# A two-layer hybrid decoder trunk: the mixers' table of chunks, side jobs and counts is replaced by another

## The chip, the core and the metric

The kernel runs on one core of a Trainium2 chip. The core has a matrix engine (TensorE: PE in the profile, PEld for its weight loads), a vector engine (VectorE, DVE), a scalar engine (ScalarE, ACT), a general engine (GpSimd, POOL) and a queue that issues DMA transfers (SyncE, SP). Each takes its own instructions in order and waits for the others by semaphores. The metric is the device time of one execution in microseconds. TensorE writes into PSUM, from which the other engines read; a PSUM buffer can be written again only when its readers are done.

## The reference

Two layers, each of three sub-layers on x (256 tokens by 1024): a gated feed-forward network (hidden width 2816) at half weight, a mixer, and a second feed-forward network at half weight. Each is wrapped in two RMS norms, x + r * post(f(pre(x))). The mixer adds two branches, each behind a sigmoid gate, and sends the sum through one output product:

```
# gated DeltaNet branch, 8 heads of 128, chunks of 64 tokens
qkv = silu(conv4(qkv));  q, k = l2norm(q), l2norm(k)
beta = sigmoid(b);  g = -exp(a_log) * softplus(a + dt_bias);  G = cumsum(g)
a_mat = strictly lower part of (k k^T * exp(G_i - G_j) * beta)
u, w  = (I + a_mat)^-1 [v * beta, k * beta * exp(G)]
per chunk: v_new = u - w state;  o = q exp(G) state + (q k^T * decay) v_new
           state = state * exp(G_last) + (k exp(G_last - G))^T v_new
o = rmsnorm(o) * silu(z)
# Conformer branch: h = a * sigmoid(gate); h = silu(layernorm(conv31(h) + dw_b))
```

All of it is float32.

## The kernel before, in words

**Weights.** Each weight matrix comes in pieces of 128 rows by 1024 columns, loaded by SP (`raw`, four buffers, line 272). ScalarE rounds a piece to `whi` (line 276) and VectorE or GpSimd makes the rest, `wlo = raw - whi` (line 280); rings of 8 hold both. A product is three matmuls, high by high, high by low, low by high. The class `Stream` decides when each step is issued; the set `POOL` says by piece number whose `wlo` GpSimd makes (53 of a mixer's pieces).

**Order of the work.** The program is straight-line. While the main line writes matmuls, a counter (`Lanes.tick`, line 212) goes up, one tick per few matmuls: in an FFN's output product, three. Side jobs (`step` of a generator up to its next `yield`) are issued when the counter has reached their due time. `DELAY` gives for each job the ticks before its first step and between the following ones, `AFTER` and `LATE` after which other jobs, and how many ticks later, it may start. `PLAN` lists the 17 column chunks in which a mixer's input product is done (g: the Conformer's gate pairs, k, q, v, z: those of DeltaNet, a and b: the branch gates, ka and kb: k with the small decay columns) and the jobs that are added when a chunk is done. `CFG` holds priorities and lags. The fillers (the taps of the long convolution on VectorE, the steps of the inverse on GpSimd) have no counts: they are issued while an engine's modelled clock is less than a set time ahead of TensorE's modelled one. `vector_us` and `pool_us` (lines 85 to 95) give these clocks their durations. What each engine does in which order is thus fixed when the program is built.

**The jobs that matter below.**
- `pre0` (lines 449 to 484): at the end of a sub-layer's output product, when the first 128 tokens are through their post norm, x times the norm weight goes into `xw`, and TensorE transposes it in two groups of four, `tr<-cst,xw`. It runs at five boundaries: FFN to mixer twice (there xw waits for the norm factor `rstd`), and mixer to FFN and FFN to FFN, three in all.
- `inv` (lines 995 to 1022): the triangular blocks are inverted on GpSimd in 31 pairs of steps on `iu`, behind `xin`, the decays and `dt`; two DMAs write the result to a buffer `dU`, eight bring it back as `u`.
- `merge` (lines 1023 to 1071): TensorE transposes u (`gd<-cst,u`) and puts the blocks together; the scans `s0`, `s1` need it.
- `cn` (lines 1268 to 1292): the layer norm behind the long convolution. Four transposes of h (`hT`) go into one PSUM buffer `tr`; VectorE takes the statistics (`bns`, `mv`), GpSimd the power -0.5 (`lnr`), VectorE writes `xhat` out of PSUM, and TensorE transposes `xhat` back; ScalarE makes `cf` of that. `tr` and the merge's `gd` have three PSUM buffers between them, the products' `mm` four.

In the profile one line, L124, stands for all VectorE and GpSimd operations, L171 for ScalarE's, L144 for matmuls and L150 for transposes; all lie 12 higher in the changed kernel.

Of the kernel before, what the change touches and what calls it, by code (L numbers as in the profile page):

```python
# [35 lines left out]


PLAN = [
# [4 lines left out]
]  # L43

DELAY = {
# [12 lines left out]
}  # L58

AFTER = {  # L60
# [9 lines left out]

FILL = (("c3", "c2", "c1", "c0"), ("inv",))

LATE = {"inv": 20, "cn": 12, "sim0": 5, "sim1": 6, "merge": 7, "dts": 14}

POOL = {*range(7, 10), *range(11, 14), 16, *range(18, 21), 22, 23, 25, *range(29, 33), 35, 36, 38, 39, *range(41, 45), *range(47, 50), 51, 53, 55, 58, 60, 61, 63, *range(65, 69), *range(70, 73), 77, 78, 85}

CFG = dict(stat=1000, conv=50, ev=300, tok=4, st=4, post=-800, pre=1000, fin=None, turn=100, tokens=-100, glu=100, dec=200, dts=500, kt=300, vt=0, qt=50, inv=1000, sim=100, merge=-400, scan=50, norm=-800, onorm=-100, yt=-400, w=50, tails=4, ahead=1.5, lag=6, free=3, aheadp=3, lag2=3, bias=2, held=1)

KIND = {"f_g0": "glu", "f_g1": "glu", "f_g2": "glu", "f_g3": "glu", "decays": "dec", "dts": "dts", "kt0": "kt", "kt1": "kt",
        "vt0": "vt", "vt1": "vt", "qt0": "qt", "qt1": "qt", "qs": "qt", "inv": "inv", "sim0": "sim", "sim1": "sim",  # L80
# [2 lines left out]


def vector_us(name, size, k):
    return 0.1 + size / 960.0


def pool_us(name, size, k):
# [88 lines left out]
class Lanes:  # L178
# [24 lines left out]
    def ready(self, job):  # L203
        late = LATE.get(job[1], 0)
        return job[2] or all(self.done.get(name, self.now) + late <= self.now and name in self.done for name in AFTER.get(job[1], ()))
# [6 lines left out]
    def tick(self):  # L212
# [5 lines left out]
        for job in list(self.jobs):  # L218
            if job in self.jobs and not any(job[1] in f for f in FILL) and job[0] <= self.now and self.ready(job):
                self.step(job)  # L220
        for eng, names, ahead in zip(self.engines, FILL, (CFG["ahead"], CFG["aheadp"])):
            while eng.at < self.pe.at + ahead:
# [109 lines left out]
def trunk(ctx: ExitStack, tc: tile.TileContext, x_in, wfirst, consts, feat, pch, tokp,  # L332
# [70 lines left out]
    for l in range(depth):  # L403
        side += [False] * 66 + [i in POOL for i in range(90)] + [False] * 66
        pieces += [w1i[l, i] for i in range(44)] + [w1o[l, i] for i in range(22)]
# [1101 lines left out]
```

## Time and profile before

| | |
|---|---|
| median of three runs | 1353.26 us (1352.9 to 1353.55) |
| profiled execution | span 1349.7 us; the page gives no other time of it, and the timed median lies 3.6 us over the span |
| TensorE busy | 1327.1 us in 7259 matmuls and transposes |
| VectorE, ScalarE, GpSimd busy | 933.8, 732.3 and 445.5 us |
| mixer 1 and mixer 2 | about 184 to 488 us and 853 to 1156 us |

A line of the page gives the code's line, the engine, the operation and its tiles (out<-in), the shapes and the count. A bracket at the end of a row of a timeline is the time for which the engine sat idle before it, and what ended that. SPq is the queue that issues DMAs.

### The profile page before, as it was taken

How to read it: one execution, taken by the hardware profiler on the slowest of the kernel's cores; microseconds unless marked ns; L12 is line 12 of the kernel's file. 1: busy time of each engine (PE TensorE's matmuls, PEld its weight loads, DVE VectorE, ACT ScalarE, POOL GpSimd, SP SyncE). 2: the span in 40 equal slices, each digit the busy share in tenths (PEclk: the TensorE clock that was granted, in tenths of full speed). 3: DMA queues.
4: the chain of work that ended last, by engine and by line, in shares of the span. 5: the costliest groups of instructions: out<-in, count | busy, mean ns of one | idle time of the engine just before them, and what ended most of it. 6: DMA issues, size and time to landing. Idle time of an engine off the chain costs nothing.

```text
span 1349.7 us, 20220 instructions
## 1 busy us (share of the span) xinstructions
PE 1327.1 (98%) x7259; PEld 1128.0 (84%) x7259; DVE 933.8 (69%) x1594; ACT 732.3 (54%) x1175; POOL 445.5 (33%) x374
## 2 busy tenths in 40 slices
PE   9999999999999999999999999999999999999998
PEld 7888889997787888888888888899977878888886
DVE  6676455999966776665576654579999666766553
ACT  7545447675555545544455543577656564555541
POOL 0111017798744201111011120277986431011110
PEclk9999999999999999999999999999999999999999
DMA  8878746562634666776468775465545446477861
GB/s 274 287 239 260 249 156 210 166 211 96 206 110 153 225 218 222 276 249 221 155 219 280 265 235 186 146 231 172 173 138 183 143 139 234 154 261 247 273 212 39
DMA packets 115652, 273.76 MB, mean 203 GB/s; under 512 B 24768, under 2 KB 48352, under 8 KB 115552
## 3 DMA queue, kind: packets, MB, share of 16 engines
q1 hardware_dynamic: 115264, 272.40, 61.5%
q8 instruction: 57, 0.93, 0.3%
q14 instruction: 43, 0.35, 0.1%
q10 hardware_dynamic: 288, 0.07, 0.0%
HBM read 256.68 MB, written 15.75 MB: 202 GB/s over the span
## 4 chain that ended last, share of the span: by engine, by line
PE 81%; DVE 11%; ACT 3%; DMA 2%; issue 1%; POOL 1%; DVEq 0%; POOLq 0%; SPq 0%; ACTq 0%
PE mm L144 75%; DVE cacc L124 4%; PE gd L144 3%; DVE c L124 3%; DVE wlo L124 2%; PE tr L150 2%; DMA raw<-mw 2%; ACT whi L171 1%; DVE at L124 1%; ACT dt L171 1%; ACT sg L171 0%; DMA raw<-w2i 0%; DVE ssk L124 0%; DVE qk L124 0%; POOL rk L124 0%
## 5 line engine op out<-in xcount | busy, mean ns | idle before, releaser
L144 PE MATMUL mm<-whi,xt 128*128 128x512 f32 (+1 forms) x2048 | 647.6, 391 | 3.0 <-ACT qT L171 2.2
L171 ACT CAST whi<-raw 128x1024 fp32r<-128x1024 f32 (+2 forms) x448 | 458.8, 1035 | 316.8 <-PE mm L144 173.8
L124 DVE TENSOR_TENSOR wlo<-raw,whi 128x1024 fp32r<-128x1024 f32 (+2 forms) x342 | 427.2, 1264 | 190.0 <-ACT whi L171 183.5
L144 PEld LDWEIGHTS mm<-whi,xt 128*128 128x128 f32 x2048 | 382.3, 188 | 82.3 <-ACT qT L171 3.0
L144 PE MATMUL mm<-wlo,xt 128*128 128x512 f32 (+1 forms) x1024 | 396.4, 387 | 0.1
L124 POOL TENSOR_TENSOR wlo<-raw,whi 128x1024 fp32r<-128x1024 f32 (+1 forms) x106 | 250.5, 2379 | 142.5 <-ACT whi L171 140.0
L144 PEld LDWEIGHTS mm<-wlo,xt 128*128 128x128 f32 x1024 | 192.6, 188 | 37.6 <-DVE wlo L124 1.3
L144 PE MATMUL mm<-whi,act 128*128 128x512 f32 x704 | 218.3, 390 | 0.0
L124 POOL TENSOR_TENSOR act<-way,act 128x512 fp32r<-128x512 f32 x44 | 79.1, 1798 | 396.1 <-ACT act L171 385.9
L124 DVE SCALAR_TENSOR_TENSOR cacc<-hT,pc,cacc 128x254 f32<-128x254 f32 (+28 forms) x464 | 179.5, 472 | 0.2
L144 PE MATMUL mm<-xt,whi 128*128 128x256 f32 x960 | 175.5, 285 | 0.8 <-ACT qT L171 0.6
L144 PEld LDWEIGHTS mm<-whi,act 128*128 128x128 f32 x704 | 132.2, 188 | 27.4
L144 PEld LDWEIGHTS mm<-xt,whi 128*128 128x128 f32 x960 | 149.4, 192 | 1.9 <-ACT qT L171 0.9
L144 PE MATMUL mm<-wlo,act 128*128 128x512 f32 x352 | 137.0, 389 | 0.0
L144 PE MATMUL mm<-xt,wlo 128*128 128x256 f32 x480 | 135.9, 283 | 0.0
L171 ACT ACTIVATE ag<-mm,rstd 128x256 f32<-128x256 f32 x88 | 41.7, 474 | 100.0 <-PE mm L144 80.5
L144 PEld LDWEIGHTS mm<-xt,wlo 128*128 128x128 f32 x480 | 92.0, 192 | 0.0
L124 DVE SCALAR_TENSOR_TENSOR ag<-mm,rstd,ag 128x256 f32<-128x256 f32 x88 | 42.3, 481 | 58.7 <-ACT ag L171 58.4
L144 PEld LDWEIGHTS mm<-wlo,act 128*128 128x128 f32 x352 | 66.1, 188 | 13.6
L124 POOL TENSOR_TENSOR rpost<-ss,exp 128x1 f32<-128x1 f32 x12 | 6.5, 538 | 193.8 <-DVE ss L124 193.8
L171 ACT ACTIVATE jk<-mm 128x512 f32<-128x512 f32 x24 | 14.3, 598 | 60.4 <-PE mm L144 60.4
L124 DVE SCALAR_TENSOR_TENSOR c<-mm,pc,c 128x255 f32<-128x255 f32 (+2 forms) x108 | 43.7, 478 | 2.6 <-ACT c L171 2.6
(187 smaller groups left out, 1148.3 us busy)
## 6 DMA issues: line engine op xcount, KB each, us to landing
raw<-mw SPq DMA_DIRECT2D x168, 512.0 KB, 3.8
raw<-w2i SPq DMA_DIRECT2D x88, 512.0 KB, 4.8
raw<-w1i SPq DMA_DIRECT2D x84, 512.0 KB, 4.9
raw<-w1o SPq DMA_DIRECT2D x44, 512.0 KB, 4.7
raw<-w2o SPq DMA_DIRECT2D x44, 512.0 KB, 4.3
way<-way SPq DMA_DIRECT2D x176, 64.0 KB, 1.8
way<-way SPq DMA_DIRECT2D x44, 256.0 KB, 4.8
wbc<-feat SPq DMA_DIRECT2D x13, 512.0 KB, 4.9
```

The source lines that it names most:

```text
L124: r = op(out, *a, **k)
L144: r = self.eng.matmul(o, w, x, **k)
L150: r = self.eng.transpose(*a)
L171: r = op(*a, **k)
```

## The change

Only tables and two constants of a model change: the order of the chunks (q0/q1, g2/g3 and b0/b1 trade places), the chunk at which nine side jobs are added, the tick counts of nearly all jobs, which jobs wait how long behind others, the pieces whose `wlo` GpSimd makes (again 53 a mixer), `free`, which ends the fixed order of VectorE's taps one chunk sooner, and VectorE's modelled duration, 0.14 us instead of 0.1 us plus the size term for steps of more than 40 elements and 0.085 us for smaller ones. The two new keys of `CFG` are read nowhere. Every engine issues the same instructions as before, in another order.

```diff
--- before.py
+++ after.py
@@ -36,25 +36,37 @@
 
 
 PLAN = [
-    ("g0", ["f"]), ("k1", ["f", "sim1"]), ("ka", ["f", "decays", "kt1", "dts"]), ("g1", ["f", "c0"]),
-    ("kb", ["f", "sim0", "kt0", "inv", "c1"]), ("g3", ["f", "c3"]), ("g2", ["f"]), ("v1", ["f", "vt1", "c2"]),
-    ("q0", ["f", "qt0", "s1"]), ("q1", ["f", "qt1", "qs", "cn"]), ("v0", ["f", "vt0"]), ("z0", ["s0"]),
-    ("z1", ["merge"]), ("a0", ["cn1"]), ("b0", []), ("b1", ["on0"]), ("a1", ["on"]),
+    ("g0", ["f"]),
+    ("k1", ["f", "sim1"]),
+    ("ka", ["f", "decays", "kt1", "dts", "c1"]),
+    ("g1", ["f", "c0", "kt0"]),
+    ("kb", ["f", "inv"]),
+    ("g2", ["f", "sim0"]),
+    ("g3", ["f"]),
+    ("v1", ["f", "vt1", "c2", "c3", "cn", "vt0"]),
+    ("q1", ["f", "qt1", "s1", "qs"]),
+    ("q0", ["f", "qt0"]),
+    ("v0", ["f"]),
+    ("z0", ["cn1"]),
+    ("z1", ["merge"]),
+    ("a0", ["s0"]),
+    ("b1", ["on0"]),
+    ("b0", []),
+    ("a1", ["on"]),
 ]
 
 DELAY = {
-    "first": (1, 1, 2, 2, 2, 2, 2), "ffn": (3, 0, 12), "pre0": (10, 7, 8, 4, 5, 3), "pre1": (15, 16, 0, 13, 8),
-    "yt0": (10, 0, 10, 10, 26), "yt1": (10, 2, 0, 3, 3), "f_g0": (3, 0, 2, 9, 1), "f_g1": (5, 1, 1, 1),
-    "c0": (0, 16, 0), "f_k1": (0, 1, 3, 1, 1, 3), "f_ka": (3, 0, 3), "decays": (12, 4, 2, 15, 4),
-    "dts": (50, 3, 0, 0, 19, 19), "kt1": (18, 3, 4, 1, 4), "sim1": (39, 0, 1, 6, 8, 15, 14, 8), "f_kb": (0, 0, 8),
-    "kt0": (4, 1, 4, 0, 4), "sim0": (16, 3, 8, 1, 3, 2, 8, 0), "inv": (76, 4, 9, 0, 14, 16, 9, 1),
-    "f_g2": (0, 1, 0, 1), "c1": (7, 0), "f_g3": (0, 1, 3, 1, 1, 1, 1), "f_v0": (1, 0, 1, 1, 0, 0, 0),
-    "vt0": (20, 0, 0, 20, 0, 37, 6, 0), "c3": (19, 20, 24, 44), "f_v1": (0, 1, 3, 0, 1, 2),
-    "vt1": (56, 12, 18, 5, 17, 2, 3, 8), "c2": (6, 0, 0, 0), "f_q0": (0, 0, 3, 1, 1, 0),
-    "merge": (4, 3, 2, 2, 2, 3, 2, 2), "qt0": (6, 0, 4, 0, 1, 0, 30, 3), "qt1": (0, 10, 28, 21, 28, 0, 17, 14),
-    "f_q1": (1, 1, 3, 1, 0, 0, 2), "qs": (0, 31, 31, 24, 19), "s0": (15, 6, 0, 0, 17, 17, 25),
-    "s1": (11, 5, 3, 6, 1, 1), "cn": (52, 20, 4, 30, 3, 0, 41, 8), "on0": (13, 5, 5, 0),
-    "on": (1, 21, 0, 0, 5, 1, 16, 16), "cn1": (0, 0, 4, 0, 6, 3, 0, 1),
+    "first": (1, 1, 2, 2, 2, 2, 2), "ffn": (3, 0, 12), "pre0": (8, 7, 3, 30, 1, 4), "pre1": (15, 0, 12, 1, 0),
+    "yt0": (10, 1, 11, 24, 0), "yt1": (10, 11, 30, 8, 12), "f_g0": (3, 3, 0, 13, 9), "f_g1": (7, 1, 0, 12), "c0":
+    (0, 8, 8), "f_k1": (4, 0, 9, 0, 4, 3), "f_ka": (3, 1, 0), "decays": (12, 4, 2, 15, 4), "dts": (49, 2, 1, 2, 12,
+    25), "kt1": (14, 3, 4, 0, 3), "sim1": (20, 0, 5, 0, 20, 29, 18, 1), "f_kb": (4, 0, 5), "kt0": (12, 0, 8, 0, 3),
+    "sim0": (18, 6, 12, 0, 3, 4, 12, 30), "inv": (75, 3, 3, 0, 14, 6, 9, 0), "f_g2": (1, 0, 3, 6), "c1": (10, 12),
+    "f_g3": (6, 3, 3, 1, 16, 4, 0), "f_v0": (0, 0, 1, 1, 4, 4, 0), "vt0": (6, 0, 19, 34, 0, 45, 3, 0), "c3": (14,
+    23, 9, 32), "f_v1": (0, 0, 6, 0, 1, 9), "vt1": (56, 12, 12, 4, 18, 10, 7, 8), "c2": (14, 15, 2, 1), "f_q0": (0,
+    8, 3, 0, 0, 8), "merge": (4, 3, 0, 6, 1, 3, 0, 2), "qt0": (3, 0, 12, 1, 0, 1, 7, 6), "qt1": (12, 6, 25, 33, 32,
+    1, 20, 13), "f_q1": (9, 1, 0, 1, 0, 0, 0), "qs": (0, 11, 28, 10, 15), "s0": (0, 0, 0, 0, 16, 30, 29), "s1": (38,
+    5, 0, 8, 16, 10), "cn": (52, 1, 4, 30, 6, 0, 26, 8), "on0": (16, 7, 5, 3), "on": (0, 19, 0, 0, 13, 1, 2, 16),
+    "cn1": (12, 0, 0, 2, 2, 6, 1, 16),
 }
 
 AFTER = {
@@ -70,11 +82,11 @@
 
 FILL = (("c3", "c2", "c1", "c0"), ("inv",))
 
-LATE = {"inv": 20, "cn": 12, "sim0": 5, "sim1": 6, "merge": 7, "dts": 14}
-
-POOL = {*range(7, 10), *range(11, 14), 16, *range(18, 21), 22, 23, 25, *range(29, 33), 35, 36, 38, 39, *range(41, 45), *range(47, 50), 51, 53, 55, 58, 60, 61, 63, *range(65, 69), *range(70, 73), 77, 78, 85}
-
-CFG = dict(stat=1000, conv=50, ev=300, tok=4, st=4, post=-800, pre=1000, fin=None, turn=100, tokens=-100, glu=100, dec=200, dts=500, kt=300, vt=0, qt=50, inv=1000, sim=100, merge=-400, scan=50, norm=-800, onorm=-100, yt=-400, w=50, tails=4, ahead=1.5, lag=6, free=3, aheadp=3, lag2=3, bias=2, held=1)
+LATE = {"inv": 15, "cn": 10, "sim0": 3, "sim1": 6, "merge": 7, "dts": 15, "vt0": 6, "kt1": 3, "vt1": 0, "qt0": 5, "kt0": 0, "s1": 3, "s0": 0, "qt1": 0}
+
+POOL = {7, 8, 9, 10, 12, 18, 19, 20, 22, 23, 25, 27, 30, 32, 35, 36, 38, 39, 41, 42, 43, 46, 47, 49, 51, 53, 54, 55, 58, 61, 63, 65, 66, 67, 68, 70, 71, 72, 76, 83, 85}
+
+CFG = dict(stat=1000, conv=50, ev=300, tok=4, st=4, post=-800, pre=1000, fin=None, turn=100, tokens=-100, glu=100, dec=200, dts=500, kt=300, vt=0, qt=50, inv=1000, sim=100, merge=-400, scan=50, norm=-800, onorm=-100, yt=-400, w=50, tails=4, ahead=1.5, lag=6, free=4, aheadp=3, lag2=3, bias=2, held=1, dv=0.14, ds=0.085)
 
 KIND = {"f_g0": "glu", "f_g1": "glu", "f_g2": "glu", "f_g3": "glu", "decays": "dec", "dts": "dts", "kt0": "kt", "kt1": "kt",
         "vt0": "vt", "vt1": "vt", "qt0": "qt", "qt1": "qt", "qs": "qt", "inv": "inv", "sim0": "sim", "sim1": "sim",
@@ -83,7 +95,7 @@
 
 
 def vector_us(name, size, k):
-    return 0.1 + size / 960.0
+    return (0.14 if size > 40 else 0.085) + size / 960.0
 
 
 def pool_us(name, size, k):
```

On TensorE, end of the first FFN, output product (`act` is the gated hidden layer, `cst` the identity that a transpose multiplies by). Before:

```order
540 L144 MATMUL mm<-wlo,act 128x512
541 L144 MATMUL mm<-whi,act 128x512 x2
542 L144 MATMUL mm<-wlo,act 128x512
543 L144 MATMUL mm<-whi,act 128x512
544 L150 MATMUL tr<-cst,xw 128x128 x4
545 L144 MATMUL mm<-whi,act 128x512
```

and in the changed kernel:

```order
536 L156 MATMUL mm<-wlo,act 128x512
537 L156 MATMUL mm<-whi,act 128x512 x2
538 L156 MATMUL mm<-wlo,act 128x512
539 L156 MATMUL mm<-whi,act 128x512
540 L162 MATMUL tr<-cst,xw 128x128 x4
541 L156 MATMUL mm<-whi,act 128x512
```

The rows before these are the same pattern of matmuls in both; the first four transposes stand four rows, six matmuls, earlier. The same holds at the other boundaries.

On GpSimd, last third of the inverse in mixer 1 (`iu<-iu,ia` forms a product, `iu<-iu` subtracts it). Before:

```order
82 L124 TENSOR_TENSOR iu<-iu 128x10x12
83 L124 TENSOR_TENSOR iu<-iu,ia 128x121
84 L124 TENSOR_TENSOR iu<-iu 128x11x11
85 L124 TENSOR_TENSOR iu<-iu,ia 128x110
86 L124 TENSOR_TENSOR iu<-iu 128x11x10
87 L124 TENSOR_TENSOR iu<-iu,ia 128x108
88 L124 TENSOR_TENSOR iu<-iu 128x12x9
89 L124 TENSOR_TENSOR iu<-iu,ia 128x96
90 L124 TENSOR_TENSOR iu<-iu 128x12x8
91 L124 TENSOR_TENSOR iu<-iu,ia 128x91
92 L124 TENSOR_TENSOR iu<-iu 128x13x7
93 L124 TENSOR_TENSOR iu<-iu,ia 128x78
```

and in the changed kernel:

```order
85 L136 TENSOR_TENSOR iu<-iu 128x11x11
86 L136 TENSOR_TENSOR wlo<-raw,whi 128x1024
87 L136 TENSOR_TENSOR iu<-iu,ia 128x110
88 L136 TENSOR_TENSOR iu<-iu 128x11x10
89 L136 TENSOR_TENSOR iu<-iu,ia 128x108
90 L136 TENSOR_TENSOR iu<-iu 128x12x9
91 L136 TENSOR_TENSOR iu<-iu,ia 128x96
92 L136 TENSOR_TENSOR iu<-iu 128x12x8
93 L136 TENSOR_TENSOR iu<-iu,ia 128x91
94 L136 TENSOR_TENSOR iu<-iu 128x13x7
95 L136 TENSOR_TENSOR wlo<-raw,whi 128x1024
96 L136 TENSOR_TENSOR iu<-iu,ia 128x78
```

Two splits of weights now stand here; between the first and the last step on `iu` there are five, where there were two. On SP, between the two `dU` transfers and the eight `u` transfers, one weight load stands now and two stood before.

On TensorE, the norm behind the long convolution in mixer 1, before (the first eight hT transposes stand at 1410 and 1411, 15 matmuls ahead of row 1423):

```order
1417 L144 MATMUL mm<-wlo,xt 128x512
1418 L144 MATMUL mm<-whi,xt 128x512 x2
1419 L144 MATMUL mm<-wlo,xt 128x512
1420 L144 MATMUL mm<-whi,xt 128x512 x2
1421 L144 MATMUL mm<-wlo,xt 128x512
1422 L144 MATMUL mm<-whi,xt 128x512
1423 L150 MATMUL tr<-cst,hT_1711 128x128 x4
1424 L150 MATMUL tr<-cst,hT_1712 128x128 x4
1425 L150 MATMUL tr<-cst,xhat 128x128 x8
1426 L144 MATMUL mm<-whi,ct 128x512
```

and in the changed kernel:

```order
1397 L162 MATMUL tr<-cst,hT_1718 128x128 x4
1398 L162 MATMUL tr<-cst,hT_1719 128x128 x4
1399 L156 MATMUL mm<-whi,xt 128x512
1400 L156 MATMUL mm<-wlo,xt 128x512
1401 L156 MATMUL mm<-whi,xt 128x512
1402 L162 MATMUL tr<-cst,hT_1718 128x128 x4
1403 L162 MATMUL tr<-cst,hT_1719 128x128 x4
1404 L156 MATMUL mm<-whi,xt 128x512
```

The second set of hT transposes moves up behind three matmuls. 12 matmuls follow, four xhat transposes, 21 matmuls and the other four.

## The prediction

> **What bounds the kernel now.** I read the page first, then TensorE's waits, then a table by stage, and last the timelines of TensorE, VectorE, GpSimd and the DMA queue at the places where TensorE waits.
>
> ```profile
> span 1349.7 us, 20220 instructions
> PE 1327.1 (98%) x7259; PEld 1128.0 (84%) x7259; DVE 933.8 (69%) x1594; ACT 732.3 (54%) x1175; POOL 445.5 (33%) x374
> PE 81%; DVE 11%; ACT 3%; DMA 2%; issue 1%; POOL 1%; DVEq 0%; POOLq 0%; SPq 0%; ACTq 0%
> ```
>
> TensorE is busy for 1327.1 of 1349.7 us and carries 81% of the chain of waits. The change issues the same instructions on every engine, so TensorE's own work stays. What can move is the 22.6 us in which it isn't busy, and any new wait. The waits, as total, times and longest, are few:
>
> ```profile
> PE tr L150 <- ACT cf L171: 3.4, 2, 1.7
> PE tr L150 <- ACT vT L171: 2.9, 2, 1.5
> PE mm L144 <- ACT qT L171: 2.8, 4, 1.1
> PE tr L150 <- ACT stg L171: 1.8, 2, 1.2
> PE gd L150 <- ACT sq L171: 1.6, 2, 1.2
> ```
>
> Each comes once or twice per mixer; the two mixers lie 668 us apart and repeat one another. By stage (length; then busy time of PE, PEld, DVE, ACT, POOL; granted clock):
>
> ```profile
> 184.00:250.00 66.00, 64.69 (x433) 58.89 (x433) 45.35 (x106) 41.04 (x70) 38.46 (x19) 1.00 0.61 196
> 250.00:300.00 50.00, 49.90 (x420) 49.72 (x419) 48.22 (x127) 36.11 (x69) 43.90 (x38) 1.00 0.61 189
> 300.00:365.00 65.00, 60.57 (x414) 52.07 (x413) 62.74 (x149) 38.31 (x78) 55.26 (x74) 1.00 0.47 151
> ```
>
> The stretch 300 to 365 loses most, 4.4 us, and there VectorE is busy for 62.7 of 65 us and GpSimd for 55.3. It is the stage in which the triangular inverse runs on GpSimd and the merge on TensorE waits for it.
>
> **The change, part by part.** A step of a side job is placed by counting matmuls; one tick of the counter inside an FFN's output product is three matmuls, and two matmuls start 0.45 us before the next one:
>
> ```profile
> 416.67 0.62 PE L144 MATMUL mm<-whi,xt 128*128 128x512 f32 x2
> 417.12 0.39 PE L144 MATMUL mm<-wlo,xt 128*128 128x512 f32 x1
> ```
>
> so a matmul takes 0.226 us in the stream.
>
> *Transposes of the normalised input (pre0).* The first count falls from 10 to 8: the first four transposes stand 6 matmuls earlier, 6 x 0.226 = 1.36 us, at all five boundaries between sub-layers. What they need, xw, comes out of a chain (sums, rstd on GpSimd, a product on VectorE) that starts from an earlier product and isn't sped up:
>
> ```profile
> 183.25 0.75 DVE L124 SCALAR_TENSOR_TENSOR xw<-x,rstd,wbc 128x512 f32<-128x512 f32 x1 [0.66 <-POOL rstd L124]
> 184.14 0.63 PE L150 MATMUL tr<-cst,xw 128*128 128x128 f32 x4
> ...
> 852.85 0.52 PE L150 MATMUL tr<-cst,xw 128*128 128x128 f32 x3 [0.19 <-DVE xw L124]
> ...
> 487.89 0.68 DVE L124 TENSOR_TENSOR xw<-x,wbc 128x512 f32<-128x512 f32 x1
> 489.31 0.60 PE L150 MATMUL tr<-cst,xw 128*128 128x128 f32 x4
> ...
> 669.57 0.69 DVE L124 TENSOR_TENSOR xw<-x,wbc 128x512 f32<-128x512 f32 x1
> 670.92 0.60 PE L150 MATMUL tr<-cst,xw 128*128 128x128 f32 x4
> ...
> 1155.60 0.68 DVE L124 TENSOR_TENSOR xw<-x,wbc 128x512 f32<-128x512 f32 x1
> 1157.02 0.60 PE L150 MATMUL tr<-cst,xw 128*128 128x128 f32 x4
> ```
>
> Ahead of mixer 1 xw ends at 183.25 + 0.75 = 184.00 and the transposes start 0.14 us later; ahead of mixer 2 (852.85) the trace names a wait for xw outright. VectorE itself waited for rstd, so no reordering on VectorE brings xw forward: there the whole 1.36 us becomes a wait, twice 2.72. At the other three the transposes start 0.74, 0.66 and 0.74 us after xw ends. Less the 0.14 us of release seen above, 0.60, 0.52 and 0.60 are slack, and 0.76, 0.84 and 0.76 are lost: 2.36. Together **+5.1 us**. Bounds: +2.7 (the three later boundaries find other cover) and +6.8 (5 x 1.36). TensorE takes its instructions in order, so all matmuls behind these transposes wait too, and nothing hides that.
>
> *The way to the merge.* The merge's first transposes need the inverse U, which goes from GpSimd through two sets of DMAs on SP:
>
> ```profile
> 250.00 1.09 ACT L171 ACTIVATE sq<-tr 128x512 f32<-128x512 f32 x2 [4.77 <-PE tr L150]
> ...
> 253.16 0.22 POOL L124 TENSOR_TENSOR xin<-xin,G 128x16 f32<-128x16 f32 x1 [4.83 <-ACT xin L171]
> ...
> 265.51 2.58 POOL L124 TENSOR_SCALAR_AFFINE_SELECT dt<-gx 128x1024 f32<-128x1024 f32 x2 [1.78 <-DMA gx<-gd]
> ...
> 299.33 0.24 POOL L124 TENSOR_TENSOR iu<-iu,ia 128x31 f32<-128x31 f32 x1
> ...
> 337.91 1.30 SPq L1014 DMA_DIRECT2D dU<-iu  x2
> 339.31 2.05 SPq L272 DMA_DIRECT2D raw<-mw  x2
> 341.51 5.30 SPq L1019 DMA_DIRECT2D u<-dU  x8
> ```
>
> and GpSimd splits weights (wlo) ahead of the inverse and inside it, 13 and 3 in these stretches of the trace:
>
> ```profile
> L124 POOL TENSOR_TENSOR wlo<-raw,whi 128x1024 fp32r<-128x1024 f32 x13 | 31.0, 2409 | 0.2
> ...
> L124 POOL TENSOR_TENSOR wlo<-raw,whi 128x1024 fp32r<-128x1024 f32 x3 | 8.2, 2734 | 0.0
> ```
>
> (the last of the three follows the inverse, so two are inside). In the changed order 13 stand ahead and 5 inside: three more inside by the order's rows, at 2.4 us each +7.2 us. Against it: the wait of 1.78 us for gx goes, since its DMA is issued one weight load earlier, and xin comes earlier, part of the 4.83 us that GpSimd sat idle; I take 1.9 us: 0.5 for one of the two sq steps (1.09 us for both) and as much for one copy, which ScalarE now does after its own xin, and 0.9 of the 1.2 us stall on stg, whose transposes the new order puts 4 ticks later, so that TensorE and all that follows it come sooner. The inverse would end at 337.9 - 1.8 - 1.9 + 7.2 = 341.4 us, where it was 337.9. Bounds: 339.5 (xin gains 3.8 of the 4.83 us) and 344.3 (xin gains nothing, and a split inside costs the 8.2 / 3 = 2.73 us of the second row).
>
> From there: SP issues dU, now one weight load instead of two (2.05 us for both), and then eight u transfers, of which the merge's first half needs four. Those land after half of 5.30 us and the median landing,
>
> ```profile
> DMA to landing us min/median/max: 1.9/4.1/5.2
> ```
>
> that is 341.5 + 2.65 + 4.1 - 337.9 = 10.3 us after the inverse before, and 9.3 now, so U is there at about 350.7 us (348.8 to 353.6). TensorE passes there at present so, in mixer 1 and 2:
>
> ```profile
> 352.32 0.66 PE L150 MATMUL gd<-cst,u 128*128 128x128 f32 x4 [1.17 <-ACT sq L171]
> ...
> 1019.74 0.66 PE L150 MATMUL gd<-cst,u 128*128 128x128 f32 x4 [0.47 <-ACT sq L171]
> ```
>
> The second is 351.65 on the first one's scale. In the new order sq's weight is loaded ahead of dU, and the conv taps of chunk v0 have less VectorE work in front, so the waits on sq, stg, qT and vT in the list above (1.6 + 1.8 + 2.8 + 2.9 = 9.1 us over both mixers, 4.6 each) have room to vanish and TensorE would be there at 352.3 - 4.6 = 347.7. Then it waits for U instead: a gain of 4.6 turns into 352.3 - 350.7 = 1.6 and 351.65 - 350.7 = 0.95; I take 350.4, by a landing a little under the median, since the first u transfers have the fewest ahead of them: 1.9 + 1.2, so **-3.1 us** in all. Bounds: -9.1 (U never late) and +3.3 (U at 353.6: 1.3 + 2.0).
>
> *The norm after the long convolution (cn).* The count between its first and second set of transposes falls from 20 to 1 and the rest is spread:
>
> ```profile
> 415.33 1.03 PE L150 MATMUL tr<-cst,hT 128*128 128x128 f32 x8
> 415.97 1.30 DVE L124 BATCH_NORM_STATS2 bns<-tr 128x6 f32<-128x512 f32 x2 [5.13 <-PE tr L150]
> 417.30 0.21 DVE L124 BATCH_NORM_AGGREGATE mv<-bns 128x2 f32<-128x12 f32 x1
> 417.78 0.55 POOL L124 TENSOR_TENSOR lnr<-lnv,exp 128x1 f32<-128x1 f32 x1 [0.74 <-DVE lnv L124]
> 418.36 1.53 DVE L124 TENSOR_SCALAR xhat<-tr,mv,lnr 128x512 f32<-128x512 f32 x2 [0.66 <-POOL lnr L124]
> ...
> 422.81 0.66 PE L150 MATMUL tr<-cst,xhat 128*128 128x128 f32 x4 [1.72 <-ACT cf L171]
> ```
>
> Now TensorE waits 1.72 us for cf before the last xhat transposes. In the new order 12 and 21 matmuls (2.7 and 4.7 us) stand ahead of the two groups of xhat transposes, so that wait goes. But tr has three PSUM buffers, and each group of four hT transposes takes one. Three matmuls after the first eight, the fourth group needs the buffer of the first, which is free when the first xhat has read it: 418.36 + half of 1.53 = 419.13, 3.8 us after the first transpose, and the third bns (0.65) now stands ahead of mv, and there is the release, 0.14: 4.6 us. TensorE is there after about 0.9 + 3 x 0.226 + 0.4 = 2.0 us, and waits 2.6 us; a split of 2.4 us that can stand in front of lnr on GpSimd in part adds some 0.3. So 2.9 in place of 1.72, **+1.2 a mixer, +2.4 us**. Bounds: -3.4 (no buffer conflict; the order excludes it unless a buffer is free that I count as taken) and +7.2 (the split wholly ahead of lnr and the release 0.3 later, 2 x (2.6 + 2.4 + 0.3 - 1.72)).
>
> *At nothing:* the swapped chunks q0/q1, g2/g3, b0/b1 (the same products by another name; the weight order changes with them), s0 hung on a0, on and on0, which stand between matmuls whose inputs exist in the stretch after the merge; only scan_first could cost there, some 0.5 us each mixer, if its copies were late. VectorE's altered clock is a number of the planner: it moves conv taps among other VectorE steps and changes no duration.
>
> **Sum:** 5.1 - 3.1 + 2.4 = +4.4 us; I take off 0.7 for waits of under 0.5 us that a longer wait just ahead absorbs. The span goes from 1349.7 to 1353.4. The timed median 1353.26 lies 3.6 us over that span, and I add the same: **1357.0 us**. Two changes within 0.2% (2.7 us) can't be told from no change here.
>
> **A rule against it.** The trace grants clock 1.00 in every stage above, with no wait longer than 1.72 us. The Trainium skill, "TensorE: Matmul & The Clock Gate", section "Part 1: The HAM clock gate (the "warmup" mystery)", says that the array falls to half clock after an idle window of about 3.4 us and needs about as long of work to return. No wait here is long enough to show it. As a mechanism of this kernel: if the new wait at cn came out as 2.6 + 2.4 = 5.0 us, and the next stretch of matmuls as long as that wait took twice 0.226 us each, 2.5 us more each mixer: 1357.0 + 2 x (2.1 + 2.5) = 1366.
>
> **Rivals.** (B) *U is in time*, the other sign: if the inverse ends by 338 us as before, U is there at 347.3, TensorE's waits of 4.6 us before the merge all vanish, and -3.1 becomes -9.1: 1351.0; 1348.6 if the three later boundaries' pre0 costs are hidden as well. For it: GpSimd's 4.83 us idle before xin is larger than what I took. Against: five splits inside the inverse. It decides from an end of the inverse before 338 us. (C) *U is late*: the inverse ends at 344.3, U at 353.6, +3.3 instead of -3.1, 1363.4. For it: GpSimd has 55.3 busy of 65 us, and 2.73 us per split inside the inverse, above the 2.41 outside. Against: the gx wait surely goes. (D) *Nothing measurable*: the counts are in planner units, other steps move along with the transposes, and gains and losses cancel: 1353.3, for which speaks that TensorE has only 22.6 us of slack and no instruction is added.
>
> **How the numbers follow.** The forecast has 0.52 (its own range 1354 to 1360; 0.36 of it lies above 1356.0), B 0.22 (0.17 below 1350.6), C 0.12, D 0.11, the clock rule 0.03. Faster: 0.17. Same: 0.16 + 0.05 + 0.11 = 0.32. Slower: 0.36 + 0.12 + 0.03 = 0.51. The range 1349.5 to 1362.0 leaves out some 0.1 of B and C's upper part with the clock rule.
>
> **What would show it.** Right: waits of 1.4 us for xw ahead of both mixers and 0.8 at the other three; at the merge a wait for u, at some 350 us, with few waits from 300 on; at cn a wait of 2.6 to 3 us before the second hT transposes, named after xhat, and none on cf. Wrong: xw finished earlier than 183; u landed before TensorE comes; an inverse that ends beyond 343; or a new wait in a stage that I priced at nothing, the scans and the output norm first.

## The result, and the profile after

The changed kernel takes 1363.97 us (median of 5 runs, 1362.29 to 1365.43), the kernel before 1352.9 us beside it: ratio 1.0087, 95% interval 1.0075 to 1.0099. It is slower by 0.87%, some 11.8 us by the ratio (the medians lie 11.1 us apart). The forecast was slower, at 1357.0 us, with a range up to 1362.0; the time lies above it.

The profiled execution of the changed kernel, from its page:

```profile
span 1363.3 us, 20238 instructions
PE 1330.9 (98%) x7259; PEld 1132.6 (83%) x7259; DVE 929.7 (68%) x1594; ACT 729.9 (54%) x1175; POOL 447.1 (33%) x374
```

Of the 13.6 us that the span has grown, only 3.8 are busy time of TensorE, with the same 7259 instructions; the rest is waiting. This execution is the longest of the five: 1365.43 us, 2.1 us over its span. In all runs here that difference is 1.8 to 2.2 us. The prediction added 3.6 us; as an estimate from these differences, the profiled execution of before lay 1.5 us under the median that it was set against. TensorE's waits (total, times, longest):

```profile
PE tr L162 <- DVE xw L136: 7.1, 5, 1.7
PE tr L162 <- DVE xhat L136: 6.3, 2, 3.1
PE mm L156 <- ACT qT L183: 4.5, 2, 2.2
PE mm L156 <- DVE c L136: 2.2, 2, 1.5
...
PE gd L162 <- DMA u<-dU: 1.3, 1, 1.3
PE tr L162 <- ACT stg L183: 1.2, 2, 0.7
```

The forecast's two new waits head the list, for xw at five boundaries and for xhat in both mixers; the old waits on cf, vT and sq are gone, and the one on qT has grown. The next fence is TensorE's timeline at the norm behind the long convolution (start, busy time of the group, count):

```profile
413.92 0.60 PE L162 MATMUL tr<-cst,hT 128*128 128x128 f32 x4
417.66 1.09 PE L162 MATMUL tr<-cst,hT 128*128 128x128 f32 x4 [3.14 <-DVE xhat L136]
418.40 0.78 PE L156 MATMUL mm<-whi,xt 128*128 128x512 f32 x1
418.97 0.63 PE L156 MATMUL mm<-wlo,xt 128*128 128x512 f32 x1
419.40 1.05 PE L156 MATMUL mm<-whi,xt 128*128 128x512 f32 x2
420.25 0.63 PE L156 MATMUL mm<-wlo,xt 128*128 128x512 f32 x1
```

The wait of 3.14 us is about the one forecast (2.9). What was not forecast stands behind it: two matmuls start 0.85 us before the next (419.40 to 420.25), where the stream does it in 0.45. The table by stage names the cause. Its columns are as in the prediction: length, busy time of PE, PEld, DVE, ACT and POOL, the granted clock, and last two of the DMA:

```profile
405.00:413.00 8.00, 8.00 (x43) 6.77 (x42) 5.24 (x14) 4.22 (x6) 2.62 (x1) 1.00 0.19 68
414.00:418.00 4.00, 0.86 (x7) 0.65 (x6) 3.30 (x7) 0.00 (x0) 2.67 (x2) 0.84 0.57 178
418.00:423.50 5.50, 5.50 (x16) 4.40 (x15) 2.82 (x6) 0.83 (x1) 0.56 (x1) 0.50 0.14 57
423.50:430.00 6.50, 6.50 (x33) 5.35 (x32) 0.76 (x2) 4.78 (x11) 4.79 (x2) 0.99 0.26 84
```

The wait cost TensorE half its clock until 423.5 us. That is the rule of the Trainium skill, "TensorE: Matmul & The Clock Gate", section "Part 1: The HAM clock gate (the "warmup" mystery)", which the prediction gave 0.03: an idle array falls to half clock and takes some 3.4 us to come back. The trace agrees with the halving (0.50). It differs in the length: a wait of 3.14 us was enough, less than the 3.4 us that the Trainium skill names. The last section has more on when the clock falls and returns.

Where the time went, from TensorE's starts in both traces, each compared with the usual step of its form (us over both layers; slow steps count with the wait ahead of them):

| place | before | after | grown by | forecast |
|---|---|---|---|---|
| xw, five boundaries | 0.7 | 7.9 | 7.3 | 5.1 |
| conv norm, cn | 3.8 | 10.5 | 6.7 | 2.4 |
| from stg to the merge | 13.2 | 12.4 | -0.8 | -3.1 |
| opening, first 11 us | 1.6 | 3.3 | 1.7 | 0 |

The four rows add up to 14.9 us; smaller differences elsewhere take 1.3 back. The opening has the same instructions in the same order in both; its matmuls step at 0.43 us for longer in this execution (see the last section).

### The profile page after: what moved, and what is told of

Its sections match the earlier page's. It is cut to its first block, busy times and chain, and to the rows that moved or that the text cites. A ratio compares the mean times of both kernels' runs of the same rounds, so it can differ in the third digit from the quotient of the medians.

```text
span 1363.3 us, 20238 instructions
## 1 busy us (share of the span) xinstructions
PE 1330.9 (98%) x7259; PEld 1132.6 (83%) x7259; DVE 929.7 (68%) x1594; ACT 729.9 (54%) x1175; POOL 447.1 (33%) x374
## 4 chain that ended last, share of the span: by engine, by line
PE 84%; DVE 8%; issue 2%; DMA 2%; POOL 2%; ACT 2%; SPq 0%; POOLq 0%; DVEq 0%; ACTq 0%
PE mm L156 78%; PE gd L156 4%; DVE cacc L136 3%; PE tr L162 2%; DVE c L136 2%; DVE wlo L136 1%; POOL wlo L136 1%; DMA raw<-mw 1%; ACT whi L183 1%; DVE qk L136 0%; PE gd L162 0%; DVE xw L136 0%; DMA raw<-w1i 0%; DVE x L136 0%; ACT jk L183 0%
## 5 line engine op out<-in xcount | busy, mean ns | idle before, releaser
L136 DVE TENSOR_TENSOR wlo<-raw,whi 128x1024 fp32r<-128x1024 f32 (+2 forms) x342 | 435.6, 1288 | 222.1 <-ACT whi L183 216.9
L156 PEld LDWEIGHTS mm<-wlo,act 128*128 128x128 f32 x352 | 66.1, 188 | 13.6
```

What stands on the lines that cost most here:

```text
L136: r = op(out, *a, **k)
L156: r = self.eng.matmul(o, w, x, **k)
```

## The experiments

The theory behind them: pre0's and cn's counts are nearly the whole loss, cn's by its wait and by the half clock behind it. Rivals: the waits only stand in for others (nothing is won by taking them away); the layout of the chunks or VectorE's modelled duration loses by itself; the slow matmuls come from the norm's stage, not from the wait. Of each edit only the entries that differ are shown, without the rest of their lines. The kernel before, beside which they ran, had medians of 1351.5 to 1352.2 us.

### pre0's count back to 10 in the changed kernel

```diff
-    "pre0": (8, 7, 3, 30, 1, 4)
+    "pre0": (10, 7, 3, 30, 1, 4)
```

> The changed kernel with pre0's first count back at 10, so that the first four xw transposes stand six matmuls later at five boundaries; nothing else is edited. Theory (the boundary waits are a loss of their own): waits for xw fall by 1.36 us at four boundaries and by 0.76 at the FFN-to-FFN one, 6.2 us in all; 0.3 to 0.5 us stay at four places, since a third split on VectorE still stands ahead of xw behind each mixer. Time about 1357.8 us. Rival (the wait only moves, to the next copies and products): no more than 2 us gained, 1362 us or above.

Measured: 1358.58 us, ratio to before 1.0051 (1.0035 to 1.0066), so 0.36% or 4.9 us less than with the change. The waits for xw fall from 7.9 us to 1.7, as expected. The six runs were far apart, 1353.81 to 1362.0. The trace of the shortest shows why: the wait at cn is there, but not the half clock behind it (one stretch at half clock comes later, at 976.9, behind the wait for qT).

```profile
411.66 0.60 PE L162 MATMUL tr<-cst,hT 128*128 128x128 f32 x4
415.39 0.63 PE L162 MATMUL tr<-cst,hT 128*128 128x128 f32 x4 [3.13 <-DVE xhat L136]
```

and by stretches of time:

```profile
411.50:415.50 4.00, 0.87 (x7) 0.57 (x6) 3.30 (x8) 0.00 (x0) 2.90 (x2) 1.00 0.56 176
415.50:421.00 5.50, 5.50 (x29) 4.61 (x29) 3.05 (x6) 2.75 (x7) 2.27 (x2) 1.00 0.16 64
```

The wait is as long, the program differs at pre0's count alone, and yet the granted clock is 1.00 (the 29 matmuls and transposes of the second row compare with 16 in as long a stretch above). Over its runs the span goes roughly with the mean granted clock: 1351.7 us at 0.998, 1355.0 at 0.996, 1355.1 and twice 1357.9 at 0.994, 1359.9 at 0.993. So a wait of one length costs the clock in one execution and not in another; the last section shows what decides.

### pre0's count to 8 in the kernel before

```diff
-    "pre0": (10, 7, 8, 4, 5, 3)
+    "pre0": (8, 7, 8, 4, 5, 3)
```

> The kernel before with pre0's first count at 8 instead of 10, nothing else. Theory: by the prediction's term the waits grow by 1.36 twice and 0.76, 0.84 and 0.76, so +5.1 us, 1358.0 us; VectorE has two splits ahead of xw behind the mixers here, so the 1.9 us of the changed kernel is not reached there. Rival (earlier transposes let the next products start earlier and win some of it back): +2 us or less, 1355 us.

Measured: 1355.19 us, ratio 1.0025 (1.0017 to 1.0034): +3.4 us. The waits are 1.66 and 1.72 us ahead of the mixers and 0.78, 0.76 and 0.78 at the other boundaries, which is the prediction's term to a tenth. Against that, the waits of 1.33, 0.63 and 0.27 us at the merge are gone, since TensorE comes there later. The term was right as a wait and lies between theory and rival as a price.

### cn's second count at 3 in the changed kernel

```diff
-    "cn": (52, 1, 4, 30, 6, 0, 26, 8)
+    "cn": (52, 3, 4, 30, 6, 0, 26, 8)
```

> The changed kernel with cn's second count at 3 instead of 1: nine matmuls stand between the first two and the last two groups of hT transposes, not three. Theory (idle TensorE long enough loses the clock): the wait falls from 3.3 to about 1.9 us, all matmuls behind it step at 0.227 us, none at 0.427; gain 1.36 twice plus the slow stretch behind it (2.9 us in mixer 1, 1.2 in mixer 2), 6.8 us in all, 1357.2 us. Rival (slow matmuls come from something else in that stage, a memory or a port that the norm loads): steps of 0.427 us remain, gain 2.7 us, 1361.2 us.

Measured: 1360.3 us, ratio 1.0061 (1.0049 to 1.0073), 0.26% or 3.5 us under the changed kernel; 6.8 was expected. At cn it went as the theory says: a wait of 1.95 us in both mixers (1.79 in the row), and full steps behind it.

```profile
416.02 0.63 PE L162 MATMUL tr<-cst,hT 128*128 128x128 f32 x4 [1.79 <-DVE xhat L136]
...
416.95 0.63 PE L156 MATMUL mm<-whi,xt 128*128 128x512 f32 x2
417.42 0.39 PE L156 MATMUL mm<-wlo,xt 128*128 128x512 f32 x1
```

But in this execution the clock fell elsewhere, behind the waits for qT of 2.67 us at 304 and 2.38 at 976. The clock is lost at waits of other stages too.

### cn's second count at 1 in the kernel before

```diff
-    "cn": (52, 20, 4, 30, 3, 0, 41, 8)
+    "cn": (52, 1, 4, 30, 3, 0, 41, 8)
```

> The kernel before with cn's second count at 1 instead of 20: three matmuls, then the last two groups of hT transposes, 12 matmuls and all eight xhat transposes. Theory: a wait of about 3.3 us for a PSUM buffer appears in each mixer, behind it matmuls step at 0.427 us for a few us, and the old wait of 1.88 us on cf goes or shrinks below 0.5; net +1.4 to +1.9 by the wait and +1 to +3 by the clock in each mixer, 1358 to 1362 us. Rival (only the wait counts): +2.8 to +3.8 us over both, 1356 to 1357 us, all steps at 0.227.

Measured: 1362.19 us, ratio 1.0077 (1.0064 to 1.0089): +10.4 us by one number. The wait for the PSUM buffer is 1.98 us here, and the wait on cf does not go: with all eight xhat transposes in one place it is 3.15 us, now ahead of the first ct product, and the clock halves behind it.

```profile
425.88 0.80 PE L144 MATMUL mm<-whi,ct 128*128 128x512 f32 x1 [3.15 <-ACT ct L171]
426.48 0.63 PE L144 MATMUL mm<-wlo,ct 128*128 128x512 f32 x1
426.90 1.05 PE L144 MATMUL mm<-whi,ct 128*128 128x512 f32 x2
427.76 0.63 PE L144 MATMUL mm<-wlo,ct 128*128 128x512 f32 x1
```

So the wait has moved along the chain of the norm (VectorE, GpSimd, VectorE, TensorE, ScalarE): its end stood where it was, and only its start had been moved.

### pre0's count at 6 in the kernel before

```diff
-    "pre0": (10, 7, 8, 4, 5, 3)
+    "pre0": (6, 7, 8, 4, 5, 3)
```

> The kernel before with pre0's first count at 6 instead of 10: the first xw transposes 12 matmuls (2.72 us) earlier, in a stage of dense matmuls with nothing of the conv norm in it. Waits by the prediction's rule: 3.0 us ahead of the two mixers, 2.1 us at the other three boundaries, together 11.6 us more, less some 1.3 us that the waits ahead of the merge gave back with pre0 at 8. Theory (a long enough wait costs the clock wherever it stands): matmuls at 0.427 us behind at least some of the waits of 3.0 us, 1.7 to 3.4 us each, so 1363 to 1368 us and runs that differ by several us. Rival (the half clock belongs to the conv norm's stage): no slow matmuls, 1361.9 us, runs within 3 us of each other.

Measured: 1365.49 us (four runs, 1364.67 to 1368.71), ratio 1.0104 (1.0085 to 1.0123). The waits are 3.02, 3.08, 2.14, 2.12 and 2.14 us as forecast. Behind the first one, where nothing of the conv norm stands, the clock falls:

```profile
183.96 0.63 PE L150 MATMUL tr<-cst,xw 128*128 128x128 f32 x4 [2.86 <-DVE xw L124]
```
```profile
183.00:186.00 3.00, 2.04 (x10) 1.76 (x11) 2.94 (x4) 0.59 (x1) 0.03 (x1) 0.85 0.79 274
186.00:190.00 4.00, 4.00 (x14) 3.19 (x13) 1.44 (x2) 1.04 (x1) 0.00 (x0) 0.68 0.44 132
190.00:195.00 5.00, 5.00 (x26) 4.12 (x25) 3.54 (x4) 4.62 (x7) 0.00 (x0) 1.00 0.39 132
```

Behind the 3.08 us at 859 it does not, and behind the 2.12 us at 674 it does. It also falls behind the old wait on vT, at 335. The rival (a matter of the norm's stage) falls.

### VectorE's modelled duration alone

In the kernel before, the new one:

```diff
-    return 0.1 + size / 960.0
+    return (0.14 if size > 40 else 0.085) + size / 960.0
```

> The kernel before with the new modelled duration of VectorE's steps alone: other taps of the long convolution stand ahead of the taps of v0 (two or four fewer at most places), nothing else moves. Theory (that constant is worth little): the wait of 1.63 us on vT shrinks by up to 0.8 us, new waits below 0.5; within 1.5 us of the kernel before. Rival (the constant is the cause of the new waits of 2.4 and 1.7 us in the changed kernel's q and v stage): these appear here, +3 to +8 us.

Measured: 1364.0 us, ratio 1.0085 (1.0071 to 1.0099). Neither the theory (within 1.5 us) nor the rival (the waits of the q and v stage) foresaw this place: TensorE waits for `at`, the similarity's product on VectorE.

```profile
275.46 1.23 DVE L124 TENSOR_TENSOR wlo<-raw,whi 128x1024 fp32r<-128x1024 f32 x1 [8.07 <-issue]
282.66 0.58 PE L144 MATMUL gd<-kT 128*128 128x128 f32 x1 [3.43 <-DVE at L124]
```

VectorE is late with `at` because it had stood idle for 8.07 us ahead of a split of weights, in both mixers; the kernel before has no such wait there. The profile names no releaser. By the order of times it was the rounded half (`whi`): ScalarE comes to its next one only at 274.34, behind the steps of the decays. So more had moved than the taps of the long convolution. All this holds up the inverse, and U is late: 2.4 us at the merge in both mixers.

In the changed kernel, the old one:

```diff
-    return (0.14 if size > 40 else 0.085) + size / 960.0
+    return 0.1 + size / 960.0
```

> The changed kernel with the old modelled duration of VectorE's steps. Theory (the order of the chunks, not the constant, makes the new waits before the v chunk): the waits of 2.4 us near 305 and 1.7 us near 320 stay within 0.7 us, the time within 2 us of the changed kernel's, about 1362 to 1365 us. Rival (the constant made them): both fall under 1 us, 1358 us or below.

Measured: 1370.96 us, ratio 1.0141 (1.0128 to 1.0155), 0.54% over the changed kernel. The waits in the q and v stage become 1.85, 2.0 and 2.7 us in each mixer. Both expectations missed. What the constant is worth depends on the table of chunks: with the old table the new value costs 11.5 us, with the new table it saves 7.3. The two fit each other, and either with the other's partner is worse than both together. "One part alone" was no measure of that part here.

### Both counts mended

```diff
-    "pre0": (8, 7, 3, 30, 1, 4), "cn": (52, 1, 4, 30, 6, 0, 26, 8)
+    "pre0": (10, 7, 3, 30, 1, 4), "cn": (52, 6, 4, 30, 6, 0, 26, 8)
```

> The changed kernel with both places mended: pre0's first count 10, cn's second count 6 (18 matmuls between the two pairs of hT groups, then 12, then 6 around the xhat groups). Theory (the change lost at two places only, and the half clock behind the wait at cn makes the runs of one kernel differ): no wait over 0.5 us at cn, none over 0.6 at the boundaries; against the profiled execution with pre0 at 10 (1351.7 us, no half clock at cn) 2 x 3.3 us less: span 1345.1, timed 1347.2 us plus 0 to 3.4 us for a half clock behind the waits of 2.4 us that stay at 304 and 973; the runs lie within 4 us of each other instead of 8.2. Rival (the waits at cn only stood in for the ones behind them): 1352 us or above.

Measured: 1354.68 us, ratio 1.0024 (1.0014 to 1.0034), 8.5 us under the changed kernel. No wait is left at the hT transposes, but a new one: 1.71 and 0.72 us for ct, since only six matmuls stand between the two xhat groups and none behind them. Behind it, and behind the 2.4 us at 974, the clock falls. The runs lie 4.3 us apart, not 8.2. The theory's 1347.2 to 1350.6 us was missed, and the time lies where the rival put it: a part of the wait came back, at the next steps of the chain.

With the counts as they were before the change, cn's at 20:

```diff
-    "pre0": (8, 7, 3, 30, 1, 4), "cn": (52, 1, 4, 30, 6, 0, 26, 8)
+    "pre0": (10, 7, 3, 30, 1, 4), "cn": (52, 20, 4, 30, 6, 0, 26, 8)
```

> The changed kernel with the two first-named counts as they were before: pre0's first count 10 and cn's second count 20 (36 matmuls, then the last hT groups and all eight xhat transposes); all else as changed. Theory (those two counts are nearly the whole of the loss, and the rest of the change is worth between 0 and +3 us): the old wait of 1.7 to 1.9 us on cf is back, no wait of 3.3 us, few slow matmuls; 1351.5 to 1354.5 us. Rival (the new layout of the chunks loses by itself): 1357 us or more.

Measured: 1352.29 us against 1352.15, ratio 1.0004 (0.9992 to 1.0015). **Two numbers make the whole difference between the kernels; all else in the change together is worth nothing that can be measured** (by the interval, between -1.1 and +2.0 us). The runs from the other side agree: in the kernel before, the two numbers cost 3.4 and 10.4 us, together 13.8, where the whole change costs 11.8. The old wait on cf (1.88 us by the starts) is back, and the waits of 2.4 and 2.7 us for qT stay, in place of those that the change took away.

### Fewer taps ahead

The twice mended kernel (cn's count 6) with one number of `CFG`:

```diff
-ahead=1.5
+ahead=0.7
```

> The kernel with both places mended (pre0 10, cn 6) and in addition the long convolution's taps allowed only 0.7 us ahead of TensorE's modelled clock instead of 1.5. Theory (the wait of 2.4 us near 304 comes from taps of the long convolution that stand ahead of q1's short-convolution taps on VectorE): that wait falls by about 0.8 us in both mixers, to 1.6, and the half clock behind it becomes rarer; 1.5 to 3 us less than without, unless taps that are left over end late, behind v0, and delay cn. Rival (the wait is set by ScalarE or by the weights): the same 2.4 us and the same time.

Measured: 1361.48 us, ratio 1.0071 (1.0058 to 1.0084), 6.4 us worse than without. The wait at 304 falls only from 2.4 to 2.06 us, and the taps that are left over end late: TensorE waits 2.35 and 5.78 us for vr, and again at cn.

### The norm begun earlier and spread

In the changed kernel, with pre0 at 10:

```diff
-    "cn": (52, 1, 4, 30, 6, 0, 26, 8)    LATE: "cn": 10
+    "cn": (45, 6, 4, 2, 6, 0, 26, 8)     LATE: "cn": 2, "cn1": 6
```

> The changed kernel with pre0's first count 10 and the conv norm begun earlier (cn may start 2 ticks after s1 instead of 10) and spread: 18 matmuls between the two pairs of hT groups, 12 and 6 around the first two xhat groups, 21 behind them, and cn1 no sooner than 6 ticks after cn. Theory (what is left of the loss in the twice mended kernel is its own new wait of 1.71 + 0.72 us for ct, because only 0 to 6 matmuls stood behind the last xhat group): these waits go, 2 x 2.4 us, and with them the half clock at 420 and 1080 to 1110; 1354.7 - 4.9 = 1349.8 us, up to 1.7 less where the half clock goes too, so 1348 to 1350, at or just under the kernel before (1351.5). Rival (the norm's chain of five engines needs its time wherever it stands, so the wait comes back at another step of it): 1353 us or more.

Measured: 1356.87 us, ratio 1.0038 (1.0026 to 1.0051), some 2 us over the twice mended kernel, with intervals that overlap, so no gain and no loss that is shown. The wait for ct is gone; in its place TensorE waits ahead of an xhat group, as the rival has it:

```profile
416.35 0.60 PE L162 MATMUL tr<-cst,xhat 128*128 128x128 f32 x4
420.20 0.63 PE L162 MATMUL tr<-cst,xhat 128*128 128x128 f32 x4 [1.85 <-DVE xhat L136]
```

In the kernel before:

```diff
-    "cn": (52, 20, 4, 30, 3, 0, 41, 8)   LATE: "cn": 12
+    "cn": (40, 6, 5, 2, 3, 0, 41, 8)     LATE: "cn": 0, "cn1": 6
```

> The kernel before with its conv norm begun earlier and spread in the same way (cn right after s1; 18, 15, 6 and 12 matmuls; cn1 6 ticks after cn), nothing else edited. Theory: its wait of 1.88 us for cf in each mixer goes, no new wait above 0.5 us; -3.8 us, 1347.7 us against 1351.5, faster by 0.25 to 0.3%. Rival (as for the other kernel: the wait comes back, or the output norm's o steps, now behind the conv norm on VectorE, are late): 1351 us or more.

Measured: 1349.54 us against 1351.62 (11 and 15 runs), ratio 0.9987 (0.9978 to 0.9996). The waits on cf of 1.88 us are gone and 0.40 us is left at ct:

```profile
421.36 0.39 PE L144 MATMUL mm<-wlo,ct 128*128 128x512 f32 x1
421.98 0.73 PE L144 MATMUL mm<-whi,ct 128*128 128x512 f32 x2 [0.23 <-DVE ct L124]
```

It beats both kernels by 0.13% and 1.0%; 1.8 us of the expected 3.8 show in the median, 3.2 in the profiled spans (1346.5 against 1349.7).

## Why the prediction was wrong, step by step

**Right:** the direction, and that the waits at the boundaries and at cn outweigh what is won before the merge. The transposes ahead of the mixers: 1.36 us each forecast, 1.36 measured (0.30 to 1.66, 0.36 to 1.72; these come from the starts, so they are a little longer than the brackets); at the FFN to FFN boundary 0.84 forecast, 0.76 measured. The wait at cn: 2.9 forecast, 3.14 in the row, and its cause, the PSUM buffer that xhat frees. The old wait on cf went.

Of the span's growth 3.7 us were forecast and 13.6 came. Of the 9.9 us between, cn holds 4.3, the way to the merge 2.3, pre0 2.2 and the opening 1.7; smaller differences take 0.6 back.

**Step that failed: cn as a wait alone.** The term was +2.4 us; it measured 6.7 in the trace. Of that 2 x (3.30 - 1.88) = 2.8 us are the wait, by TensorE's starts, and the other 3.9 the half clock behind it. The prediction had the rule as a rival, with a point from which it decides that lay too high: a wait of 5.0 us, where 3.1 was enough. It read from the trace of before that waits up to 1.72 us leave the clock alone, which is so in that trace, and let the 3.4 us of the Trainium skill stand for the gap between.

**Step that was short: pre0 behind the mixers.** 0.76 us each was forecast, 1.90 came, so that pre0 cost 7.3 us in all and not 5.1. The step counted the slack of xw on the old order of VectorE. In the new order one more split stands ahead of xw there:

```profile
491.74 3.52 DVE L136 TENSOR_TENSOR wlo<-raw,whi 128x1024 fp32r<-128x1024 f32 x3
495.18 0.69 DVE L136 TENSOR_TENSOR xw<-x,wbc 128x512 f32<-128x512 f32 x1
```
```profile
496.01 0.63 PE L162 MATMUL tr<-cst,xw 128*128 128x128 f32 x4 [1.74 <-DVE xw L136]
```

The three splits take 3.52 us, where the rows of before had two in 2.35: 1.17 us, and 0.76 + 1.17 = 1.93.

**Step that failed: the way to the merge.** -3.1 us was forecast, -0.8 measured. In this execution TensorE stands 3.0 us behind the one of before when mixer 1 has begun (1.7 from the opening, 1.36 at xw), so 3.0 is taken off here for the scale of before. GpSimd's timeline:

```profile
254.21 0.22 POOL L136 TENSOR_TENSOR xin<-xin,G 128x16 f32<-128x16 f32 x1 [5.90 <-PE mm L156]
...
273.46 2.42 POOL L136 TENSOR_TENSOR wlo<-raw,whi 128x1024 fp32r<-128x1024 f32 x1 [1.02 <-ACT whi L183]
...
302.97 0.24 POOL L136 TENSOR_TENSOR iu<-iu,ia 128x31 f32<-128x31 f32 x1 [1.41 <-DMA ia<-dA]
```

xin came 2.0 us sooner (251.2 for 253.2; 1.9 forecast) and the wait for gx was gone, as forecast. But the inverse began at 300.0, where it began at 299.3 before: GpSimd now waited 1.7 us in all for ScalarE's half of the weights (whi) and 1.41 us for `ia`, a transfer that the prediction did not follow. From there on the three more splits cost what was forecast (five took 12.95 us where two took 5.81), while the steps on `iu` took 1.5 us less than before. SP issued dU, and TensorE took u, at

```profile
347.14 1.31 SPq L1026 DMA_DIRECT2D dU<-iu  x2
```
```profile
354.21 0.63 PE L162 MATMUL gd<-cst,u 128*128 128x128 f32 x4 [0.79 <-ACT whi L183]
...
1029.76 0.63 PE L162 MATMUL gd<-cst,u 128*128 128x128 f32 x4 [1.28 <-DMA u<-dU]
```

so the inverse ended at 344.1 on the scale of before, 2.7 us later than forecast and past the 343 that the prediction named as a sign against it. U was saved by its transfers:

```profile
DMA to landing us min/median/max: 1.9/2.2/2.8
```

They landed after 2.2 us, not 4.1, and the merge passed at 351.2, 1.1 us sooner than before, where 1.9 was forecast; in mixer 2 the trace names u as what TensorE waited for. What was won at sq and vT was lost at a place that the prediction had at nothing, the swapped q chunks: VectorE does 17 taps of the long convolution (cacc) and a split (wlo) among q1's taps (c), and TensorE waits.

```profile
295.70 6.37 DVE L136 SCALAR_TENSOR_TENSOR cacc<-hT,pc,cacc 128x239 f32<-128x239 f32 x17
301.99 2.41 DVE L136 SCALAR_TENSOR_TENSOR c<-mm,pc,c 128x255 f32<-128x255 f32 x6
304.33 1.21 DVE L136 TENSOR_TENSOR wlo<-raw,whi 128x1024 fp32r<-128x1024 f32 x1
305.46 2.41 DVE L136 SCALAR_TENSOR_TENSOR c<-mm,pc,c 128x255 f32<-128x255 f32 x6
```
```profile
308.02 0.47 PE L156 MATMUL mm<-xt,whi 128*128 128x256 f32 x2 [2.23 <-ACT qT L183]
```

That the taps cause this wait is read from the trace; the run with fewer taps ahead took only 0.3 us off it, so it is not shown.

**Rivals.** C (U late) had the inverse's end (344.1 against its 344.3), not its price, since the u transfers landed sooner. That C's 1363.4 us lies nearest to the measured time is luck: its cause, a late U, is a small part of what the trace shows. The clock rule had the right mechanism, and B's condition, an inverse that ends by 338, did not come. D (gains and losses cancel) describes all of the change except two numbers, as the run with both counts restored shows.

## What to carry to other kernels

In a kernel that TensorE bounds, price a new wait at its length and, from about 2 us, at a further 1.7 us or more for each time it costs the clock; two short waits some way apart are cheaper than one long one of the same sum. When a step is moved earlier, look at what stands ahead of its inputs on the engines that make them, in the new order. Before a change with many parts is judged, take out those whose waits the trace names first: here two counts out of a whole table held all of the loss.

## What the runs showed of the hardware

**The clock falls after waits well under 3.4 us, and not after each.** From all fourteen profiles, each wait of TensorE of 1.2 us or more, with the mean granted clock from the middle of the wait to 8 us behind it (halved: below 0.97; waits that follow one another closely can share a fall):

| wait, us | waits | followed by a half clock |
|---|---|---|
| 1.2 to 1.6 | 16 | 0 |
| 1.6 to 2.0 | 50 | 5 |
| 2.0 to 2.8 | 27 | 15 |
| over 2.8 | 13 | 9 |

**A fixed beat decides.** In each of the fourteen traces all changes of the granted clock lie a whole number of times 3.413 us apart: in the changed kernel at 416.76, 423.59, 1092.60 and 1096.01 us, the third 198 beats behind the first. Where the beat lies differs from execution to execution. That agrees with the Trainium skill, "TensorE: Matmul & The Clock Gate", section "Part 1: The HAM clock gate (the "warmup" mystery)", by which the window runs freely and doesn't start with the kernel. Cut at these beats, the wait at cn reads so in the changed kernel (length, then busy time of PE; the clock stands before the last two columns):

```profile
413.35:416.76 3.41, 1.17 (x8) 0.76 (x6) 2.71 (x9) 0.25 (x1) 2.99 (x2) 1.00 0.54 184
416.76:420.17 3.41, 2.51 (x8) 2.24 (x9) 2.53 (x5) 0.00 (x0) 0.18 (x1) 0.50 0.47 154
420.17:423.59 3.42, 3.42 (x9) 2.53 (x8) 1.53 (x2) 0.92 (x1) 0.38 (x1) 0.50 0.00 0
```

and so with pre0 at 10:

```profile
410.26:413.67 3.41, 2.00 (x15) 1.59 (x13) 3.38 (x11) 1.05 (x1) 2.26 (x1) 1.00 0.74 263
413.67:417.08 3.41, 1.69 (x10) 1.51 (x11) 2.58 (x6) 0.00 (x0) 0.72 (x2) 1.00 0.45 157
417.08:420.50 3.42, 3.42 (x19) 2.83 (x18) 1.63 (x3) 2.25 (x5) 1.77 (x2) 1.00 0.01 2
```

In the first, 2.24 us of one beat are idle, and the next runs at half clock. In the second the edge of a beat splits the wait into 1.41 and 1.72 us, and the clock stays. Over all fourteen traces, without the opening and the end, each of the 22 beats at full clock with more than 1.95 us of idle TensorE was followed by one at half clock, 4 of the 27 with 1.58 to 1.95, and none of the other 5337. A beat at half clock was the last one where at most 0.54 us of it were idle (26 times) and was followed by another where 0.90 or more were (6 times). A lone fall thus takes one beat, 3.41 us at half rate, 1.7 us lost; it shows as 0.89 in a stretch of 15 us (0.11 x 15 = 1.65).

**Part of the spread of a kernel's runs comes from this.** With two waits of 3.3 us and two of 2.4 (pre0 at 10), six runs lay 8.2 us apart; what their mean clocks of 0.998 and 0.993 leave out of full rate is 2.7 us in the shortest and 9.5 in the longest, an estimate from rounded figures. The kernel before, with waits up to 1.9 us, stayed within 3.9 us over 17 runs beside it, but lay 7.4 us apart over 14 later ones with clocks of 0.996 to 1.000, so the clock is not all of it.

**The opening.** Over the first 10 us the granted clock reads 1.00 in both profiles, while the matmuls step at 0.43 us for part of it (0.85 us for the two at 419.40 is that same step). The reason is that a trace's clock records begin only with the first change to full clock, at 4.87 us before and 10.57 us after. In the other twelve traces it comes at 4.08 to 7.14 us. So the 1.7 us of the opening look like a matter of this one execution and not of the change.
